# Prompt scores of two heads on two halves of the tensor array, with one split of keys and queries per pair

## The chip, the cores and the metric

The kernel runs on one core of one Trainium2 chip. The time is device microseconds of one execution; the number compared is the median of several runs. A profile of one execution gives the start and length of nearly every instruction on the five engines: TensorE (PE, with PEld for its weight loads), VectorE (DVE), ScalarE (ACT), GpSimd (POOL) and SyncE (SP, which here only issues DMAs).

## The reference

The reference is one inference step of a two-layer streaming encoder in float32: a convolution layer with its SwiGLU feed-forward, then a shared key/value projection, an attention layer with 16 heads of 64 features, a second feed-forward and a final norm. There are 512 new prompt frames and 8 running streams of 16 frames. The part that matters here is the attention of the prompt frames:

```python
def one_chunk(args):
    c, q_blk = args
    start = c * CHUNK
    k_blk = lax.dynamic_slice_in_dim(kp, start, BAND, axis=1)
    v_blk = lax.dynamic_slice_in_dim(vp, start, BAND, axis=1)
    s = jnp.einsum("bqhd,bkhd->bhqk", q_blk, k_blk).astype(jnp.float32) * scale + bias
    valid = (start - BAND_LEFT + jnp.arange(BAND)) >= 0
    s = jnp.where(valid[None, None, None, :], s, NEG_INF)
    p = jax.nn.softmax(s, axis=-1).astype(v_blk.dtype)
    return jnp.einsum("bhqk,bkhd->bqhd", p, v_blk)
```

For 512 frames in chunks of 64 with eight chunks to the left this is causal attention by chunks: each 128-frame tile of queries i (0 to 3) meets the keys 0 to (i+1)*128.

## The kernel before, in words

All matrix products run in the one-pass float32 format (`F32R`). To keep float32 accuracy each operand is split into a high part (rounded by a copy on ACT) and a low part (the difference, taken on DVE), and a product is the sum of high-high, high-low and low-high. In the projections and the feed-forwards that is three matmuls per tile (`mm3`, lines 196 to 202, and `product`, line 439).

The heads are worked on in eight pairs p. A tile of 128 partitions holds the keys of both heads of a pair, head 0 in partitions 0 to 63 and head 1 in 64 to 127 (`kts[p]`), and another the queries (`qts[p]`). They come from `proj_kq` (line 1200), the values from `proj_v` (line 1222, one call for two pairs).

`head_a(p, hh)` (line 1259) computes the prompt scores of one head and their softmax. Since a head has only 64 features, it fills all 128 rows of the array by stacking. `KK` holds the high part of the keys twice, once in each half of the partitions (an ACT copy at line 1271, then a POOL copy to the other half at line 1273). `KL` holds the low part twice (two DVE subtractions, line 1275). `QQ` holds the high part of the queries in one half (ACT, line 1272) and the low part in the other (DVE, line 1277). Then for each query tile, in the order 3, 2, 0, 1, two matmuls over all 128 rows give the sum of all four part products: `QQ` with `KK` (line 1285) and `QQ` with `KL` (line 1286). Widths are 512, 384, 128 and 256 columns. `KK`, `KL` and `QQ` have one buffer each (`KB = 1`). The scores of tiles 3, 2 and 0 go to one two-bank PSUM tile of the pool `w2` (`wide`), those of tile 1 into a spare part of a second one (`st`), which afterwards takes the scores of the sample streams. The pool `w2` has two such tiles in all. `addmax` on DVE (line 1194) adds the bias and takes the row maximum; `softmax_rows` runs the exponentials on ACT (line 1187); line 1296 divides on DVE.

The other steps of a pair are: `samp_a` (sample scores against the cache, lines 1342 and 1345, 32 array columns per stream), `head_b` (transposes of the prompt weights, line 1309), `pair_c` (prompt weights times values, line 1326, 64 array columns per head), `samp_b` (transposes, lines 1358 and 1364), and `samp_c` (sample weights times values, lines 1378 and 1382, then a transpose at 1391). All of these but `samp_a` write into the PSUM pool `am`, which has two one-bank tiles. The string `BO` (line 67) gives the written order of a pair: a0 s0 a1 s1 b0 b1 t0 n0 p0 c0 d0 t1 n1 c1 d1; `BL` is that of the last pair, with parts of the output projection put between.

The order in which the engines really receive the instructions is made by the framework's scheduler. It takes, among the instructions that are ready on its own clock, the one written first, and hands out the buffers of a pool as they come free. So the projections for the next pair, written after the pair, fill TensorE wherever the attention of this pair is waiting. Within an engine the resulting order is fixed, and semaphores hold the dependencies.

Of the kernel before, what the change touches and what calls it, by code (L numbers as in the profile page):

```python
# [8 lines left out]
F32 = mybir.dt.float32  # L9
F32R = mybir.dt.float32r  # L10
I32 = mybir.dt.int32
AF = mybir.ActivationFunctionType
ALU = mybir.AluOpType
PSUM = bass.MemoryType.PSUM

P = 128
# [6 lines left out]
DH = 64  # L23
# [32 lines left out]
NXA, NXB = NB * SEG + HIST + HA, HIST + 320  # L56
SSQ = 'avavavaa'
SCUT = 8
CB, QB, KB = 8, 1, 1
NSTD = 3  # L60
NH = NT // 2
X11, X21, XT2, XT1, XT3, XT4, X22 = range(7)
# [20 lines left out]
def tile_trunk(ctx, tc, xT, vecs, hist, w_pw1, w_pw2, w_in0, w_out0, w_os0, w_in1, w_out1, w_os1,  # L83
               w_kq, w_v, w_o, rel, kc, vc, y_out, convp_out, convs_out, k_out, v_out):
    nc = tc.nc
# [15 lines left out]
    def nm(s):  # L101
        uid[0] += 1
        return f"{s}_{uid[0]}"

    def mmt(n=512):
        return mm.tile([P, n], F32, tag="mm", name=nm("mm"))

    def w2t():
        return w2.tile([P, 1024], F32, tag="w2", name=nm("w2"))
# [761 lines left out]
    def conv_pe(c, part):  # L871
        w4, xa, xb = x4s[c]
        pt = mmt()
        n = {"S": NB * SB, "A": HA, "B": NH}[part]
        for tg in range(8):
            r = 96 if tg == 7 else P
            for q in range(4):
                if part == "S":
                    mv = xa[0:r, q, 0:NSC].rearrange("p (s w) -> p s w", w=SEG)
# [7 lines left out]
            yield  # L887
        o = {"S": 0, "A": NB * SB, "B": NH}[part]
        to_y(c, o, n, pt, func=AF.Identity, bias=col(V_BDW, c))
# [231 lines left out]
    def amt():  # L1121
        return am.tile([P, 512], F32, tag="am", name=nm("am"))

    sp = at.enter_context(tc.tile_pool(name="sp", bufs=2))
    ap = at.enter_context(tc.tile_pool(name="ap", bufs=1))

    qbd = []
    for i in range(2):
        q = ap.tile([P, NB, 2, SB], F32, name=f"qbd{i}", tag=f"qbd{i}")
# [11 lines left out]
    for b in range(4):  # L1141
        for hh in range(2):
# [3 lines left out]
                                      ap=[[0, 16], [2 * L, NP]]))  # L1146
# [33 lines left out]

    def softmax_rows(S, mx, sm, tiles):
        k = len(tiles)
# [15 lines left out]
    fill, step_end = None, [None]  # L1198
# [57 lines left out]

    ORD = (3, 2, 0, 1)

    def head_a(p, hh):
        kt, qt = kts[p], qts[p]  # L1260
        r = slice(hh * DH, hh * DH + DH)
        S = sp.tile([P, 1280], F32, tag="S", name=nm("S"))
        mx = ap.tile([P, 4], F32, tag="mx", name=nm("mx"), bufs=3)
        sm = ap.tile([P, 4], F32, tag="sm", name=nm("sm"), bufs=3)
        wide = w2t()
        st = w2t()
        ro = slice(DH - hh * DH, 2 * DH - hh * DH)
        KK = ap.tile([P, 512], F32R, tag="KK", name=nm("KK"), bufs=KB)
        KL = ap.tile([P, 512], F32R, tag="KL", name=nm("KL"), bufs=KB)
        QQ = ap.tile([P, 512], F32R, tag="QQ", name=nm("QQ"), bufs=KB)  # L1270
        nc.scalar.activation(out=KK[r], in_=kt[r, P:], func=AF.Copy)
        nc.scalar.activation(out=QQ[r], in_=qt[r, P:], func=AF.Copy)
        nc.gpsimd.tensor_copy(KK[ro], KK[r].bitcast(F32))
        for to in (r, ro):
            nc.vector.tensor_tensor(out=KL[to], in0=kt[r, P:], in1=KK[r].bitcast(F32),
                                    op=ALU.subtract)
        nc.vector.tensor_tensor(out=QQ[ro], in0=qt[r, P:], in1=QQ[r].bitcast(F32),
                                op=ALU.subtract)
        pss = []
        for i in ORD:  # L1280
            n = (i + 1) * P
            o = SOFF[i]
            q = slice(i * P, (i + 1) * P)
            ps = st[:, 640:896] if i == 1 else wide[:, o:o + n]
            nc.tensor.matmul(ps, QQ[:, q], KK[:, 0:n], start=True, stop=False)
            step_end[0] = nc.tensor.matmul(ps, QQ[:, q], KL[:, 0:n], start=False, stop=True).ins
            pss.append(ps)
        for ii, i in enumerate(ORD):
            n = (i + 1) * P
            o = SOFF[i]  # L1290
            addmax(S[:, o:o + n], pss[ii], BP[:, hh, 512 - n:512], mx[:, ii:ii + 1])
        rs = softmax_rows(S, mx, sm, [(SOFF[i], (i + 1) * P) for i in ORD])
        for ii, i in enumerate(ORD):
            n = (i + 1) * P
            o = SOFF[i]
            nc.vector.tensor_scalar(out=S[:, o:o + n], in0=S[:, o:o + n],
                                    scalar1=rs[:, ii:ii + 1], scalar2=None, op0=ALU.mult)
        return S, st

    def head_b(S):  # L1300
        PT = sp.tile([P, 1280], F32, tag="PT", name=nm("PT"))
        for kk in ((0,), (1, 3), (2,)):
            tr = amt()
            base = POFF[kk[0]]
            tot = 0
            for k in kk:
                for i in range(k, 4):
                    o = POFF[k] - base + (i - k) * P
                    step_end[0] = nc.tensor.transpose(
                        tr[:, o:o + P], S[:, SOFF[i] + k * P:SOFF[i] + (k + 1) * P], ident).ins  # L1310
                    tot += P
            if kk[0] == 0:
                nc.scalar.activation(out=PT[:, base:base + tot], in_=tr[:, :tot], func=AF.Copy)
            else:
                nc.vector.tensor_copy(PT[:, base:base + tot], tr[:, :tot])
        return PT
# [14 lines left out]
    def samp_a(p, u, st):  # L1331
        qb, kt = qbd[p % 2], kts[p]
        cache = []
        for src in (kc[p, u], vc[p, u].rearrange("p b k d -> p b (k d)")):
            for i in range(2):
                t = ap.tile([P, 2, 512], F32, tag="cache", name=nm("cache"), bufs=CB)
                nc.sync.dma_start(t, src[:, 2 * i:2 * i + 2, :])
                cache.append(t)
        KC, VC = cache[:2], cache[2:]
        qv = [qb[:, 4 * u + b, :, :].rearrange("p h q -> p (h q)") for b in range(4)]  # L1340
        for b in range(4):
            nc.tensor.matmul(st[32 * b:32 * b + 32, 0:512], qv[b], KC[b // 2][:, b % 2, :],
                             start=True, stop=True)
        for b in range(4):
            step_end[0] = nc.tensor.matmul(st[32 * b:32 * b + 32, 512:576], qv[b],
                                           kt[:, 64 * u:64 * u + 64], start=True, stop=True).ins
        S = ap.tile([P, 576], F32, tag="Ss", name=nm("Ss"), bufs=2)
        mx = ap.tile([P, 4], F32, tag="mx", name=nm("mx"), bufs=3)
        sm = ap.tile([P, 4], F32, tag="sm", name=nm("sm"), bufs=3)
        addmax(S, st[:, 0:576], BS, mx[:, 0:1])  # L1350
        rs = softmax_rows(S, mx, sm, [(0, 576)])
        return S, rs, VC
# [65 lines left out]
    for p in range(NP):  # L1418
        bias_load(p)
        if p < NP - 1:  # L1420
            oT[p] = (op_.tile([P, NT], F32R, tag="ohi", name=nm("ohi"), bufs=3),
                     op_.tile([P, NT], F32R, tag="olo", name=nm("olo"), bufs=3))
        else:
            oT[p] = (op_.tile([P, NT], F32, tag="kt", name=nm("ohi"), bufs=2).bitcast(F32R),
                     op_.tile([P, NT], F32, tag="qt", name=nm("olo"), bufs=QB).bitcast(F32R))
        ha, sa, pt, ps = {}, {}, {}, {}
        for op in (BL if p == NP - 1 else BO).split():
            i = int(op[1])
            if op[0] == "a":
                ha[i] = head_a(p, i)  # L1430
            elif op[0] == "s":
                sa[i] = samp_a(p, i, ha[i][1])
            elif op[0] == "b":
                pt[i] = head_b(ha[i][0])
            elif op[0] == "t":
                ps[i] = samp_b(i, sa[i][0])
            elif op[0] == "n":
                ps[i] = ps[i]()
            elif op[0] == "c":
                ps[i] = samp_c(p, i, ps[i], *sa[i][1:])  # L1440
            elif op[0] == "d":
                ps[i]()
            elif op[0] in "oq":
                if fill is None:
                    fill = halves(i, (mmt,), [])
                for _ in range(1 + (op[0] == "o")):
                    with tc.issue_after(step_end[0]):
                        next(fill)
            else:
                pair_c(p, (pt[0], pt[1]))  # L1450
        if p + 1 < NP:
            run(proj_kq(p + 1))
        if p % 2 == 1 and p + 1 < NP:
            run(proj_v(p // 2 + 1))
        if p in PO:
            proj_o(PO[p])
# [6 lines left out]
    with tc.high_priority(offset=HP):  # L1463
        sqs = xp.tile([P, KT, 384], F32, tag="xl1", name=nm("sqs")).rearrange("p a n -> p (a n)")
        acc, r = sqs[:, KT * NH:(KT + 1) * NH], sqs[:, (KT + 1) * NH:(KT + 1) * NH + 8]
        for k in range(KT):
            sq = square(h[:, k, 0:NH], NH, "a", sqs[:, k * NH:(k + 1) * NH])
            if k:
                sq_end = nc.vector.tensor_tensor(out=acc, in0=acc if k > 1 else sqs[:, 0:NH],
                                                 in1=sq, op=ALU.add).ins  # L1470
    for _ in range(MEAN_AT):
        next(fin)
    with tc.issue_after(half_end[0]), tc.high_priority(offset=HP):
        st, nt = w2t(), len(tiles(NH))
        for t, c in enumerate(tiles(NH)):
            end = nc.tensor.matmul(st[:, 512 + t:513 + t], acc[:, c:c + P], onec, start=True,
                                   stop=True)
# [109 lines left out]
    with tc.high_priority(offset=HP):  # L1587
        squares(0)
        st = mmt()
# [98 lines left out]
```

## Time and profile before

| what | value |
|---|---|
| median of 3 runs | 1460.51 us (1458.16 to 1463.31) |
| the profiled execution, its span | 1460.0 us |
| TensorE busy | 1434.0 us (98%) |
| VectorE busy | 1138.9 us (78%) |
| ScalarE busy | 757.8 us (52%) |
| GpSimd busy | 297.6 us (20%) |
| granted TensorE clock | 0.999 |

The page gives no time of the profiled execution beyond its span. Busy time is the union of the instructions' intervals; matmuls overlap their neighbours in the pipeline, so that the length of one matmul is longer than its share, and the distance between two starts is the better measure of its cost. A form such as `128*64 128x512` on a matmul means 128 array rows by 64 array columns in use and an output 512 wide. The attention stage runs from about 690 to 1005 us.

### The profile page before, as it was taken

How to read it: one execution, taken by the hardware profiler on the slowest of the kernel's cores; microseconds unless marked ns; L12 is line 12 of the kernel's file. 1: busy time of each engine (PE TensorE's matmuls, PEld its weight loads, DVE VectorE, ACT ScalarE, POOL GpSimd, SP SyncE). 2: the span in 40 equal slices, each digit the busy share in tenths (PEclk: the TensorE clock that was granted, in tenths of full speed). 3: DMA queues.
4: the chain of work that ended last, by engine and by line, in shares of the span. 5: the costliest groups of instructions: out<-in, count | busy, mean ns of one | idle time of the engine just before them, and what ended most of it. 6: DMA issues, size and time to landing. Idle time of an engine off the chain costs nothing. (4 is left out here: it accounts for less than half of the span.)

```text
span 1460.0 us, 28194 instructions
## 1 busy us (share of the span) xinstructions
PE 1434.0 (98%) x11022; PEld 1369.6 (94%) x11022; DVE 1138.9 (78%) x2520; ACT 757.8 (52%) x1628; POOL 297.6 (20%) x349
## 2 busy tenths in 40 slices
PE   9999999999999999999999999999999999999998
PEld 8998799999999999999987898878999999999998
DVE  6789867988888888756768668577898888888765
ACT  4666554654554554545654355443554564455453
POOL 5699120010111111013222121011011111111101
PEclk9999999999999999999999999999999999999999
DMA  7267434045444534425556554452125444444522
GB/s 243 73 180 187 126 86 146 14 135 150 131 108 118 163 92 135 116 88 193 181 163 213 173 192 162 138 200 67 44 82 143 135 113 129 137 120 109 155 66 72
DMA packets 66932, 192.56 MB, mean 132 GB/s; under 512 B 12144, under 2 KB 30320, under 8 KB 58480
## 3 DMA queue, kind: packets, MB, share of 16 engines
q1 hardware_dynamic: 52432, 160.58, 33.8%
q0 software_dynamic: 13504, 29.37, 9.9%
q8 instruction: 86, 1.41, 0.4%
q10 hardware_dynamic: 864, 0.83, 0.2%
q14 instruction: 46, 0.38, 0.1%
HBM read 179.14 MB, written 11.61 MB: 131 GB/s over the span
## 5 line engine op out<-in xcount | busy, mean ns | idle before, releaser
L439 PE MATMUL mm<-XH,whi 128*128 128x320 f32 x896 | 275.9, 310 | 2.9 <-ACT t L451 2.6
L439 PE MATMUL mm<-XH,wlo 128*128 128x320 f32 x896 | 276.1, 309 | 0.0
L439 PE MATMUL mm<-XL,whi 128*128 128x320 f32 x896 | 274.5, 309 | 0.0
L371 ACT ACTIVATE whi<-raw 128x512 fp32r<-128x512 f32 (+2 forms) x280 | 168.4, 613 | 135.2 <-PE mm L439 103.6
L199 PE MATMUL mm<-xh,whi 128*128 128x320 f32 (+2 forms) x640 | 200.2, 314 | 0.8 <-DVE h L702 0.4
L200 PE MATMUL mm<-xh,wlo 128*128 128x320 f32 (+2 forms) x640 | 198.2, 311 | 0.0
L372 DVE TENSOR_TENSOR wlo<-raw,whi 128x512 fp32r<-128x512 f32 (+2 forms) x280 | 183.9, 666 | 15.9 <-ACT whi L371 14.8
L201 PE MATMUL mm<-xl,whi 128*128 128x320 f32 (+2 forms) x640 | 195.9, 311 | 0.4 <-DVE xl L189 0.4
L439 PE MATMUL mm<-hid,whi 128*128 128x320 f32 x732 | 172.5, 311 | 5.5 <-DVE hid L372 3.1
L439 PEld LDWEIGHTS mm<-XH,whi 128*128 128x128 f32 x896 | 167.7, 188 | 4.9 <-ACT t L451 4.2
L439 PEld LDWEIGHTS mm<-XH,wlo 128*128 128x128 f32 x896 | 168.2, 188 | 0.0
L439 PEld LDWEIGHTS mm<-XL,whi 128*128 128x128 f32 x896 | 167.7, 188 | 0.0
L439 PEld LDWEIGHTS mm<-hid,whi 128*128 128x128 f32 x732 | 125.0, 188 | 8.8 <-DVE hid L372 4.2
L199 PEld LDWEIGHTS mm<-xh,whi 128*128 128x128 f32 x640 | 120.5, 188 | 4.0 <-ACT xh L187 1.5
L201 PEld LDWEIGHTS mm<-xl,whi 128*128 128x128 f32 x640 | 119.7, 188 | 1.2 <-DVE xl L189 0.8
L200 PEld LDWEIGHTS mm<-xh,wlo 128*128 128x128 f32 x640 | 120.5, 189 | 0.2
L439 PE MATMUL mm<-hid,wlo 128*128 128x320 f32 x366 | 113.0, 309 | 0.0
L439 PE MATMUL mm<-XH,slo 128*128 128x320 f32 x344 | 106.0, 308 | 0.0
L439 PE MATMUL mm<-XH,shi 128*128 128x320 f32 x344 | 105.8, 309 | 0.0
L439 PE MATMUL mm<-XL,shi 128*128 128x320 f32 x344 | 105.6, 308 | 0.0
L417 POOL DMA_DIRECT2D s<-in_w_in x38 | 22.1, 581 | 388.7 <-DVE wlo L372 151.8
L841 POOL TENSOR_TENSOR ca<-ca,cvt 128x512 f32<-128x512 f32 x60 | 91.9, 1532 | 17.8 <-ACT cvt L838 11.2
(275 smaller groups left out, 3370.8 us busy)
## 6 DMA issues: line engine op xcount, KB each, us to landing
raw<-in_w_in SPq DMA_DIRECT2D x38, 1024.0 KB
s<-in_w_in POOLq DMA_DIRECT2D x76, 256.0 KB, 4.2
raw<-in_w_os SPq DMA_DIRECT2D x24, 768.0 KB
cache<-in_ck SPq DMA_DIRECT2D x32, 512.0 KB
cache<-in_cv SPq DMA_DIRECT2D x32, 512.0 KB
raw<-in_w_pw SPq DMA_DIRECT2D x11, 1024.0 KB
s<-in_w_os POOLq DMA_DIRECT2D x48, 192.0 KB, 3.6
raw<-in_w_kq SPq DMA_DIRECT2D x8, 1024.0 KB
```

The costliest lines, as they stand in the source:

```text
L199: nc.tensor.matmul(ps, wh, xh, start=(first and i == 0), stop=False)
L200: nc.tensor.matmul(ps, wl, xh, start=False, stop=False)
L201: end = nc.tensor.matmul(ps, wh, xl, start=False, stop=(stop and i == last))
L371: put_end[1] = nc.scalar.activation(out=hi, in_=src, func=AF.Copy).ins
L372: put_end[0] = nc.vector.tensor_tensor(out=lo, in0=src, in1=hi.bitcast(F32), op=sub).ins
L417: nc.gpsimd.dma_start(s1, src[:, 2 * n:3 * n])
L439: last = nc.tensor.matmul(pt, wt, v, start=(first and k == i == 0), stop=(k == n - 1 and i == 2), skip_group_check=True)
L841: nc.gpsimd.tensor_tensor(out=acc, in0=acc, in1=pr, op=ALU.add)
```

## The change

`head_a` is cut in two. A new function `heads_split(p)` is called once per pair, ahead of head 0. It splits the keys and the queries of both heads in one go, over all 128 partitions: two ACT copies, two DVE subtractions, nothing on POOL. Then it issues the scores of both heads: per query tile three matmuls per head (high-high, low-high, high-low), each over the 64 rows of its head, the two heads taking turns. The low-low product is no longer computed. Head 0 uses rows 0 to 63 of the array, head 1 rows 64 to 127. The scores of tiles 3, 2 and 0 go to two `w2` tiles, one per head, and those of tile 1 to two tiles of the pool `am`. The sample scores get a `w2` tile of their own when their turn comes. `head_a` keeps the bias, the maximum and the softmax.

```diff
-CB, QB, KB = 8, 1, 1
+CB, QB = 8, 1
...
-    def head_a(p, hh):
+    def heads_split(p):
         kt, qt = kts[p], qts[p]
-        r = slice(hh * DH, hh * DH + DH)
-        S = sp.tile([P, 1280], F32, tag="S", name=nm("S"))
-        mx = ap.tile([P, 4], F32, tag="mx", name=nm("mx"), bufs=3)
-        sm = ap.tile([P, 4], F32, tag="sm", name=nm("sm"), bufs=3)
-        wide = w2t()
-        st = w2t()
-        ro = slice(DH - hh * DH, 2 * DH - hh * DH)
-        KK = ap.tile([P, 512], F32R, tag="KK", name=nm("KK"), bufs=KB)
-        KL = ap.tile([P, 512], F32R, tag="KL", name=nm("KL"), bufs=KB)
-        QQ = ap.tile([P, 512], F32R, tag="QQ", name=nm("QQ"), bufs=KB)
-        nc.scalar.activation(out=KK[r], in_=kt[r, P:], func=AF.Copy)
-        nc.scalar.activation(out=QQ[r], in_=qt[r, P:], func=AF.Copy)
-        nc.gpsimd.tensor_copy(KK[ro], KK[r].bitcast(F32))
-        for to in (r, ro):
-            nc.vector.tensor_tensor(out=KL[to], in0=kt[r, P:], in1=KK[r].bitcast(F32),
-                                    op=ALU.subtract)
-        nc.vector.tensor_tensor(out=QQ[ro], in0=qt[r, P:], in1=QQ[r].bitcast(F32),
-                                op=ALU.subtract)
-        pss = []
+        KH, KL, QH, QL = (ap.tile([P, 512], F32R, tag=t, name=nm(t)) for t in ("KH", "KL", "QH", "QL"))
+        for src, hi, lo in ((kt, KH, KL), (qt, QH, QL)):
+            nc.scalar.activation(out=hi, in_=src[:, P:], func=AF.Copy)
+            nc.vector.tensor_tensor(out=lo, in0=src[:, P:], in1=hi.bitcast(F32), op=ALU.subtract)
+        wide = [w2t(), w2t()]
+        narrow = [amt(), amt()]
+        pss = [[], []]
         for i in ORD:
             n = (i + 1) * P
             o = SOFF[i]
             q = slice(i * P, (i + 1) * P)
-            ps = st[:, 640:896] if i == 1 else wide[:, o:o + n]
-            nc.tensor.matmul(ps, QQ[:, q], KK[:, 0:n], start=True, stop=False)
-            step_end[0] = nc.tensor.matmul(ps, QQ[:, q], KL[:, 0:n], start=False, stop=True).ins
-            pss.append(ps)
+            for hh in range(2):
+                pss[hh].append(narrow[hh][:, 0:n] if i == 1 else wide[hh][:, o:o + n])
+            for j, (a, b) in enumerate(((QH, KH), (QL, KH), (QH, KL))):
+                for hh in range(2):
+                    r = slice(hh * DH, hh * DH + DH)
+                    step_end[0] = nc.tensor.matmul(pss[hh][-1], a[r, q], b[r, 0:n], start=j == 0,
+                                                   stop=j == 2).ins
+        return pss
+
+    def head_a(p, hh, pss):
+        S = sp.tile([P, 1280], F32, tag="S", name=nm("S"))
+        mx = ap.tile([P, 4], F32, tag="mx", name=nm("mx"), bufs=3)
+        sm = ap.tile([P, 4], F32, tag="sm", name=nm("sm"), bufs=3)
...
-        return S, st
+        return S
...
             if op[0] == "a":
-                ha[i] = head_a(p, i)
+                if i == 0:
+                    pss = heads_split(p)
+                ha[i] = head_a(p, i, pss[i])
             elif op[0] == "s":
-                sa[i] = samp_a(p, i, ha[i][1])
+                sa[i] = samp_a(p, i, w2t())
             elif op[0] == "b":
-                pt[i] = head_b(ha[i][0])
+                pt[i] = head_b(ha[i])
```

## The prediction

> **What bounds the kernel now.** I read the page first: shares of busy time, then the slices.
>
> ```profile
> span 1460.0 us, 28194 instructions
> ...
> PE 1434.0 (98%) x11022; PEld 1369.6 (94%) x11022; DVE 1138.9 (78%) x2520; ACT 757.8 (52%) x1628; POOL 297.6 (20%) x349
> ...
> PE   9999999999999999999999999999999999999998
> ...
> PEclk9999999999999999999999999999999999999999
> ```
>
> TensorE is busy in every slice and its clock is never cut. The attention stage is no exception; the view of busy time by stretches gives it one row (stretch, its length, then busy time of PE, PEld, DVE, ACT and POOL):
>
> ```profile
> 690.00:1005.00 315.00, 310.25 (x2798) 270.23 (x2797) 218.71 (x654) 157.73 (x424) 57.27 (x95) 1.00 0.51 169
> ```
>
> So 4.75 of 315 us are left uncovered on TensorE, with DVE at 69% and ACT at 50%. What the change takes from DVE, ACT and POOL can pay only through these few microseconds; what it does to TensorE's own time counts in full. That is the first cut of the sum. The timeline of TensorE shows the scores of one head (start, length, line, form):
>
> ```profile
> 763.14 0.39 PE L1285 MATMUL w<-KK,QQ 128*128 128x512 f32 x1
> 763.38 0.40 PE L1286 MATMUL w<-KL,QQ 128*128 128x512 f32 x1
> 763.61 0.34 PE L1285 MATMUL w<-KK,QQ 128*128 128x384 f32 x1
> 763.78 0.34 PE L1286 MATMUL w<-KL,QQ 128*128 128x384 f32 x1
> 763.96 0.22 PE L1285 MATMUL w<-KK,QQ 128*128 128x128 f32 x1
> 764.02 0.27 PE L1286 MATMUL w<-KL,QQ 128*128 128x128 f32 x1
> 764.13 0.33 PE L1285 MATMUL w<-KK,QQ 128*128 128x256 f32 x1
> 764.30 0.28 PE L1286 MATMUL w<-KL,QQ 128*128 128x256 f32 x1
> 764.42 0.28 PE L199 MATMUL mm<-xh,whi 128*128 128x256 f32 x1
> ```
>
> The reader should look at the distances of the starts. A matmul costs 0.235 us at 512 columns (763.14 to 763.61, halved), 0.175 at 384, and 0.12 at 256 (764.30 to 764.42). At 128 columns the first takes 0.06 and the next 0.11. I read 0.11 as the floor that a weight load sets when each narrow matmul needs new weights, and 0.17 for the first 256 as the same load arriving late. The head takes 764.42 - 763.14 = 1.28 us, a pair 2.56, eight pairs 20.5 us: 1.4% of the span is all that the change can touch directly on TensorE.
>
> **The change on TensorE.** Per pair 16 matmuls over 128 rows go, 24 over 64 rows come. If the two heads, on different halves of the rows and in different PSUM banks, run at the same time, a pair of them costs one distance, and a query tile three: 3 x (0.235 + 0.175 + 0.11 + 0.12) = 1.92 us instead of 2.56. If they run one after another it is twice that, 3.84. No row of before has both row halves at work, so these are the two bounds. The nearest rows are the sample scores, four streams on four column quarters:
>
> ```profile
> 699.94 0.28 PE L201 MATMUL mm<-xl,whi 128*128 128x256 f32 x1
> 700.06 0.28 PE L199 MATMUL mm<-xh,whi 128*128 128x256 f32 x1
> 700.27 1.07 PE L1342 MATMUL w<-cache,qbd 128*32 128x512 f32 x8
> 701.16 0.29 PE L1345 MATMUL w<-kt,qbd 128*32 128x64 f32 x8
> 701.38 0.39 PE L200 MATMUL mm<-xh,wlo 128*128 128x256 f32 x1
> 701.60 0.28 PE L201 MATMUL mm<-xl,whi 128*128 128x256 f32 x1
> ```
>
> ```profile
> 700.27 0.16 PEld L1342 LDWEIGHTS w<-cache,qbd 128*32 128x32 f32 x8
> ```
>
> Eight matmuls of 512 columns take 701.16 - 700.27 = 0.89 us, where eight in a row would take 8 x 0.235 = 1.88 at the least, and their eight weight loads start within a fraction of a microsecond. Parts of the array do work at once in this kernel. I take the overlap, 1.92, since this is the nearest row, and keep 3.84 for the range.
>
> The same rows price the second term: going into a divided array and out of it. Before the sample scores the distance is 700.27 - 700.06 = 0.21 instead of the 0.12 just ahead: 0.09 lost. After them, the 64-column round starts at 701.16 and lasts two rounds of 0.89 / 2 / 8 = 0.056, so 0.11 of the 0.22 to 701.38 are lost; and the first whole-array matmul takes 0.22 instead of 0.12, another 0.10. One trip costs about 0.30 us. Today's scores are whole-array work like the projections around them and pay nothing of the kind. So the number of blocks into which the scheduler cuts the 24 matmuls decides the sign: one block gives 1.92 + 0.30 - 2.56 = -0.34 per pair, -2.7 us in all; two give -0.04 and -0.3 us; three give +0.26 and +2.1 us.
>
> I take two. The last query tile is written into `am`, whose two tiles also serve all transposes and both value products, so it has to wait for these to be emptied while the tiles 3, 2 and 0 are free to go. Already now, the last width is cut off by projections when its PSUM tile comes late:
>
> ```profile
> 772.78 0.28 PE L1286 MATMUL w<-KL,QQ 128*128 128x128 f32 x1
> ...
> 774.32 0.28 PE L1285 MATMUL w<-KK,QQ 128*128 128x256 f32 x1
> ```
>
> A third block is possible because the high-high matmuls need only the two ACT copies and can be issued ahead of the DVE subtractions. A trip next to the sample work, which has already divided the array, would cost less; I leave that at nothing.
>
> **The change on the other engines.** From the groups by line and shape (count | busy, mean ns of one | idle before):
>
> ```profile
> L1275 DVE TENSOR_TENSOR KL<-kt,KK 64x512 fp32r<-64x512 f32 x32 | 24.0, 749 | 4.9 <-ACT KK L1271 4.5
> L1277 DVE TENSOR_TENSOR QQ<-qt,QQ 64x512 fp32r<-64x512 f32 x16 | 11.0, 685 | 1.1 <-ACT QQ L1272 0.9
> L372 DVE TENSOR_TENSOR wlo<-raw,whi 128x512 fp32r<-128x512 f32 x30 | 20.3, 683 | 1.0 <-ACT whi L371 0.9
> L1272 ACT ACTIVATE QQ<-qt 64x512 fp32r<-64x512 f32 x16 | 9.8, 615 | 0.0
> L371 ACT ACTIVATE whi<-raw 128x512 fp32r<-128x512 f32 x30 | 18.4, 628 | 9.5 <-PE mm L439 8.5 <-DVE h L580 0.6 <-DVE raw L425 0.4
> L1273 POOL CAST KK<-KK 64x512 fp32r<-64x512 f32 x16 | 14.3, 894 | 127.4 <-ACT KK L1271 126.0 <-issue 1.3
> ```
>
> A half-height subtraction costs as much as a whole one. Per pair DVE drops 4 x 0.749 + 2 x 0.685 = 4.37 us and gains 2 x 0.683 = 1.37: 3.0 us less, 24 us over the stage. ACT goes from about 4 x 0.62 to 2 x 0.628, 1.2 us less per pair. POOL loses both copies, and with them the wait on ACT at the head of its queue, behind which the bias scaling of the next pair stood. No DMA is added or moved. All of this lies beside TensorE; its worth is bounded by the waits that TensorE really has. The timeline shows the larger ones (in brackets: idle, and on whom):
>
> ```profile
> 752.58 0.39 PE L199 MATMUL mm<-whi,xh 128*128 128x256 f32 x1 [0.52 <-ACT vt L1234]
> ...
> 794.87 0.44 PE L1309 MATMUL am<-ident,S 128*128 128x128 f32 x2 [0.41 <-DVE PT L1315]
> 795.70 0.66 PE L1358 MATMUL am<-ident,Ss 128*128 128x128 f32 x4 [0.39 <-ACT PT L1313]
> ```
>
> ```profile
> L1285 PE MATMUL w<-KK,QQ 128*128 128x512 f32 x16 | 7.0, 440 | 1.3 <-DVE QQ L1277 1.2
> ```
>
> These add up to 0.52 + 0.41 + 0.39 + 1.2 = 2.5 us. That is the upper bound of the relief.
>
> Against it stands a new wait. Both `am` tiles are held from the last score matmul until head 1's last `addmax`. Behind them wait the transposes, the value products and, through those, the output projection. One head's four `addmax` run like this:
>
> ```profile
> 733.03 0.69 DVE L1194 CUSTOM_DVE_ANT_0 S<-w,BP 128x512 f32<-128x512 f32 x1 [0.92 <-PE w L1286]
> ...
> 734.68 0.08 DVE L1194 DVE_READ_ACCUMULATOR2_ANT mx<- 128x1 f32 x1
> ```
>
> That is 1.73 us, so 3.46 for two heads. The sample scores wait too: their `w2` tile is free only after the head's first three `addmax`. Head 1's scores now stand ahead of the first sample scores on TensorE; before they came after them. The cover for all this is the projections of the next pair:
>
> ```profile
> L199 PE MATMUL mm<-xh,whi 128*128 128x384 f32 x112 | 38.7, 346 | 0.0
> L199 PE MATMUL mm<-whi,xh 128*128 128x256 f32 x142 | 40.6, 286 | 0.5 <-ACT vt L1234 0.5
> ```
>
> Each line stands for three matmuls, so these two groups alone are 112 x 3 x 0.175 + 142 x 3 x 0.12 = 110 us, 13.7 per pair, against 3.46 to be hidden. I cost the hold at nothing while they are there, the relief at nothing as well, and keep +13.8 us (half of the hold bare in each pair) and -2.5 us for the range.
>
> **The sum.** Profiled 1460.0, two blocks per pair -0.3: 1459.7. The median of the runs lies 0.5 above the profiled span, so **1460.2 us**: no change that could be measured. About 0.3%, or 4.4 us, is what runs of this kernel can tell apart.
>
> **Rivals.** First, the halves do not overlap. For it speaks that no row shows both at work, against it the column quarters. With two trips a pair takes 3.84 + 0.60 instead of 2.56: 8 x 1.88 = 15.0 us, **1475.5**; with one trip 12.6, 1473.1.
>
> Second, slower by the hold: the scheduler places the last tile's scores ahead of the previous pair's value product, and that product then waits for two heads of `addmax` with no projection between. It decides from the point where TensorE's next instruction needs an `am` tile and the projections have run dry. Half the hold bare costs 8 x 1.73 = 13.8: **1474**. Against it: 13.7 us of cover per pair; for it: the waits at 794.87 and 795.70, where it already happens in small.
>
> Third, the overlap is partial: the matmuls overlap, but the weight loads of the two halves follow one another at 0.11 each, so no pair of matmuls is under 0.22. Then 3 x (0.235 + 3 x 0.22) = 2.69, plus 0.60, less 2.56: +0.73 per pair, **1466.3**; with one trip 1463.9. For it speaks the 0.11 floor above, against it the eight loads at 700.27. [...]
>
> Fourth, faster: one block per pair (-2.7) and all of TensorE's listed waits gone (-2.5): **1455.3**. For it: 24 us less on DVE; against it: the `am` tiles.
>
> **How the numbers follow.** Forecast 0.50, with its own range 1456.5 to 1464 (one block and some relief, to three blocks and a little waiting). Not overlapping 0.13, the hold 0.16, partial overlap 0.07, faster 0.14. Faster by over 0.3% (under 1456.1) takes most of the fourth rival and a sliver of the forecast: 0.15. Slower by over 0.3% (over 1464.9) takes the first rival, most of the second and third, and an edge of the forecast: 0.34. Within: 0.51. The range 1455 to 1475 cuts through the first rival and the fourth and leaves about 0.15 out.
>
> **What would show it.** Rows `64*128` on TensorE whose starts come in twos, a few ns apart, with the next two 0.235 us later at 512 columns, show the overlap; equal distances of 0.235 refute it. At 128 columns, 0.11 per two says that loads overlap, 0.22 that they do not. Projections between `64*128` rows count the blocks. Idle time of lines 1309 and 1326 put down to line 1194 would show the hold. I would be wrong if TensorE's uncovered time in the stage grew from 4.75 us to over 9, or if the scores of a pair, trips included, left the span of 2.2 to 2.8 us.

## The result and the profile after

The changed kernel takes 1478.92 us (median of 4 runs, 1476.75 to 1479.29); the kernel before took 1460.95 us beside it (4 runs, 1458.16 to 1463.31). The ratio is 1.0126 with a 95% interval of 1.0114 to 1.0138: 18 us slower. The forecast was 1460.2 us with a range of 1455 to 1475, so the forecast and its range were both wrong.

The page of the changed kernel, beside the one shown of before (span, busy time by engine):

```profile
span 1474.9 us, 28213 instructions
...
PE 1446.4 (98%) x11086; PEld 1370.6 (93%) x11086; DVE 1119.6 (76%) x2488; ACT 746.1 (51%) x1612; POOL 282.3 (19%) x333
```

TensorE is busy for 12.4 us more and the span is 14.9 us longer; the profiled execution is the fastest of the four, so that the profile shows a little less than the 18 us. DVE and ACT did become lighter (by 19.3 and 11.7 us), and no run shows that it bought anything. The row of busy time for the attention stage of the changed kernel:

```profile
690.00:1020.00 330.00, 321.81 (x2842) 270.18 (x2841) 193.79 (x615) 144.49 (x400) 44.67 (x80) 0.99 0.48 158
```

Uncovered time is 330.00 - 321.81 = 8.19 us, where it was 4.75. From the first score matmul to the start behind the last attention matmul the stage took 307.8 us before (694.8 to 1002.6) and takes 325.1 us now (692.6 to 1017.7). It begins 2.2 us earlier and ends 15.1 us later, which is the whole difference of the spans. So TensorE's own time rose by far more than its idle time. The timeline of the changed kernel shows the scores of the first pair (start, length, line, form, count):

```profile
692.37 0.28 PE L201 MATMUL mm<-wlo,xh 128*128 128x256 f32 x1
692.58 0.50 PE L1277 MATMUL w<-KH,QH 64*128 64x512 f32 x2
...
693.03 0.40 PE L1277 MATMUL w<-KH,QL 64*128 64x512 f32 x2
693.26 0.39 PE L1277 MATMUL w<-KL,QH 64*128 64x512 f32 x2
693.49 0.33 PE L1277 MATMUL w<-KH,QH 64*128 64x384 f32 x2
693.66 0.34 PE L1277 MATMUL w<-KH,QL 64*128 64x384 f32 x2
...
694.07 0.28 PE L1277 MATMUL w<-KH,QL 64*128 64x128 f32 x2
694.19 0.27 PE L1277 MATMUL w<-KL,QH 64*128 64x128 f32 x2
694.30 0.33 PE L1277 MATMUL am<-KH,QL 64*128 64x256 f32 x2
694.47 0.28 PE L1277 MATMUL am<-KL,QH 64*128 64x256 f32 x1
694.67 0.39 PE L199 MATMUL mm<-whi,xh 128*128 128x256 f32 x1
...
697.74 0.38 PE L1277 MATMUL am<-KL,QH 64*128 64x256 f32 x1
```

Each row with x2 is the two heads, and the next row comes 0.23 us later at 512 columns, 0.17 at 384 and 0.12 at 128 (693.03 to 693.26, 693.49 to 693.66, 694.07 to 694.19). The kernel before has 0.235, 0.175 and 0.11 for one matmul over the whole array (763.14 to 764.13), so the halves run at the same time. From 692.58 to 694.67 23 of the pair's 24 matmuls cost 2.09 us, and 2.28 with the 0.09 lost ahead of them and the 0.10 behind, against 2.56 before: up to here the change does what it was meant to do. But the last matmul of one head comes alone, at 697.74, and costs another 0.51 us with the trip around it (697.53 to 698.28, less the 0.24 of two projections). And this first pair is the best of the eight. Here is the second pair:

```profile
723.19 0.28 PE L201 MATMUL mm<-xl,whi 128*128 128x256 f32 x1
723.40 0.50 PE L1277 MATMUL w<-KH,QH 64*128 64x512 f32 x2
723.83 0.44 PE L199 MATMUL mm<-xh,whi 128*128 128x384 f32 x1
...
728.22 0.50 PE L1277 MATMUL w<-KH,QL 64*128 64x512 f32 x2
...
729.48 0.28 PE L1277 MATMUL w<-KL,QH 64*128 64x128 f32 x2
729.69 0.44 PE L199 MATMUL mm<-xh,whi 128*128 128x384 f32 x1
...
743.47 0.33 PE L1388 MATMUL am<-ident,os 128*128 128x128 f32 x1
743.73 0.38 PE L1277 MATMUL am<-KH,QH 64*128 64x256 f32 x1
...
747.59 0.28 PE L201 MATMUL mm<-wlo,xh 128*128 128x256 f32 x1
747.80 0.38 PE L1277 MATMUL am<-KH,QH 64*128 64x256 f32 x1
748.02 0.28 PE L1277 MATMUL am<-KH,QL 64*128 64x256 f32 x1
748.14 0.28 PE L1277 MATMUL am<-KL,QH 64*128 64x256 f32 x1
748.35 0.39 PE L199 MATMUL mm<-whi,xh 128*128 128x256 f32 x1
748.57 0.28 PE L200 MATMUL mm<-whi,xl 128*128 128x256 f32 x1
```

The pair's scores are in four blocks instead of one. The two high-high matmuls go alone, ahead of the subtractions (723.40); 0.43 us pass until the next start, for work worth 0.23. Then come tiles 3, 2 and 0 (728.22 to 729.69). The last tile, in `am`, comes 14 us later, one head at a time: head 0 right behind line 1388, the last transposes of the previous pair, and head 1 another 4.07 us later. Two heads that start 4 us apart overlap nothing. The block at 747.80 also shows what one trip costs: the distance ahead of it is 0.21 instead of 0.12, that of its first matmul 0.22, that of its last 0.21, and that of the first whole-array matmul 0.22. Together 0.38 us are lost. This pattern of the last tile repeats in seven of the eight pairs, in six of them with other work between the heads.

Counted over the timeline of the stage, there are 34 blocks of scores (23 before), 4.25 per pair; TensorE goes from one way of dividing the array to another 170 times (103 before); and the scores take 25.7 us from start to start (21.3 before), 3.2 us per pair instead of 2.66. The groups of waits of TensorE in this stage (engine, tile, line, awaited: us in total, times, longest):

```profile
PE am L1306 <- DVE PT L1312: 1.8, 4, 0.8
PE w L1339 <- DMA cache<-in_ck: 1.7, 1, 1.7
...
PE am L1277 <- DVE mx L1194: 0.5, 1, 0.5
```

No wait stands out. The one that the forecast named, for `addmax` (line 1194), is 0.5 us in all.

### The profile page after: what moved, and what is told of

It reads as the page before. It is cut to its first block, busy times and chain, and to the rows that moved or that the text cites. A ratio compares the mean times of both kernels' runs of the same rounds, so it can differ in the third digit from the quotient of the medians.

```text
span 1474.9 us, 28213 instructions
## 1 busy us (share of the span) xinstructions
PE 1446.4 (98%) x11086; PEld 1370.6 (93%) x11086; DVE 1119.6 (76%) x2488; ACT 746.1 (51%) x1612; POOL 282.3 (19%) x333
```

## The experiments

The two theories of the expectations: **A**, the loss is the price of the divided array, the trips into and out of it; **B**, the loss is the last tile's place in `am`, which ties the scores to the tail of the previous pair. The stage is again measured from the first score matmul to the start behind the last attention matmul; it begins at 691.1 to 696.8 us, latest in e6 and e10. Uncovered time is that of TensorE from 690 to 1035 us, the same stretch for all, which takes in a little of the next stage. The kernel before was run beside each group of runs and took 1459.0 to 1459.8 us (1460.95 beside the change).

| kernel | median us | ratio to before (95%) | stage us | changes of the array's division | score blocks | uncovered us |
|---|---|---|---|---|---|---|
| before | 1460.95 | | 307.8 | 103 | 23 | 5.5 |
| the change | 1478.92 | 1.0126 (1.0114 to 1.0138) | 325.1 | 170 | 34 | 8.6 |
| e1_am | 1486.84 | 1.0190 (1.0175 to 1.0205) | 334.7 | 112 | 21 | 21.2 |
| e2_half_st | 1469.47 | 1.0071 (1.0056 to 1.0086) | 317.7 | 157 | 31 | 8.5 |
| e3_trips | 1478.06 | 1.0131 (1.0113 to 1.0148) | 327.1 | 205 | 24 | 3.7 |
| e5_one_block | 1490.15 | 1.0209 (1.0191 to 1.0226) | 340.6 | 128 | 13 | 23.4 |
| e8_mm_plain | 1469.00 | 1.0065 (1.0050 to 1.0080) | 316.6 | 145 | 27 | 10.3 |
| e6_mm_block | 1469.49 | 1.0068 (1.0051 to 1.0085) | 313.8 | 124 | 13 | 12.9 |
| e10_mm_first | 1468.69 | 1.0063 (1.0048 to 1.0078) | 313.6 | 114 | 13 | 14.1 |
| e11_whole | 1466.83 | 1.0059 (1.0044 to 1.0074) | 314.4 | 108 | 25 | 12.5 |
| e12_mm_whole | 1460.50 | 1.0006 (0.9997 to 1.0016) | 309.4 | 116 | 22 | 7.6 |

**e3_trips: what a trip costs.** The kernel before, with one tiny matmul over 64 rows behind each tile's scores, 64 in all:

```diff
             pss.append(ps)
+            nc.tensor.matmul(st[:, 960:964], QQ[0:DH, q], KK[0:DH, 0:4], start=True, stop=True)
```

> The kernel before with 64 matmuls added, one after each query tile's two score matmuls of each head, over 64 rows and 4 columns wide, into a spare part of the sample tile; nobody reads them. Each is a trip into the row-divided array and back. It measures the price of a trip: at the 0.30 us read off the column-divided rows, 64 trips cost 19 us, 1480 us in all. Theory A expects 1475 to 1485; if a trip between whole rows and half rows costs far less than one to columns (theory B), the time stays under 1468.

Measured 1478.06 us, 18.3 more than the 1459.77 of before beside it. The timeline of e3_trips:

```profile
693.53 0.40 PE L1286 MATMUL w<-KL,QQ 128*128 128x512 f32 x1
693.86 0.27 PE L1288 MATMUL w<-KK,QQ 64*128 64x4 f32 x1
694.06 0.44 PE L1285 MATMUL w<-KK,QQ 128*128 128x384 f32 x1
694.34 0.34 PE L1286 MATMUL w<-KL,QQ 128*128 128x384 f32 x1
```

The way in costs 0.33 - 0.235 = 0.095, the tiny matmul itself 0.20, and the first whole-array matmul behind it 0.28 - 0.175 = 0.105 too much: 0.40 in all, with the tiny matmul in it. The 64 added matmuls made 102 more changes of the division, not 128. So the 18.3 us are 0.18 for each change, and the 19.3 us by which the stage grew are 0.19: a trip of two changes costs 0.36 to 0.38, as in the block at 747.80 of the changed kernel. How much of it is the tiny matmul's own, this run does not separate. A trip into row halves costs somewhat more than the 0.30 that the forecast had read from the column quarters; above all it was the number of trips that was wrong.

**e1_am: the last tile in `am`, the array not divided.** The kernel before, whose last tile goes to `am`:

```diff
-        st = w2t()
+        narrow = amt()
...
-            ps = st[:, 640:896] if i == 1 else wide[:, o:o + n]
+            ps = narrow[:, 0:n] if i == 1 else wide[:, o:o + n]
...
-                sa[i] = samp_a(p, i, ha[i][1])
+                sa[i] = samp_a(p, i, w2t())
```

> The kernel before with one part of the change alone: the scores of the last query tile go to a tile of the pool am and the sample scores get a w2 tile of their own; all scores stay whole-array, each head is split and scored by itself. Theory A (the extra 18 us are trips into and out of the divided array, and matmuls of one head that run alone): no trip is added, so the time stays at that of before, 1461 us within 3. Theory B (the am tiles held by the scores make TensorE wait): most of the loss is here, 1470 us or more, and TensorE's idle time in the attention stage grows from 4.75 us to over 8.

Measured 1486.84 us, 27 more than before, with next to no added changes of the array (112 against 103). So a place in `am` can cost this much with no divided array at all, and A alone falls. But the size can't be carried over. In this kernel `KK`, `KL` and `QQ` have one buffer each, so when head 0's last tile waits for `am`, head 1's split waits for head 0's operands. Its waits of TensorE:

```profile
PE w L1285 <- POOL BP L1154: 4.7, 1, 4.7
PE w L1285 <- POOL BP L1157: 4.7, 1, 4.7
```

These two, 9.4 us, are waits that the changed kernel doesn't have. Its granted clock is down too, to 0.97 on the mean from 690 to 1035 us, which costs up to 0.03 x 345 = 10 us. This run is no clean measure.

**e2_half_st: the change, with the last tile back in the sample's tile.** The last tile's three half-row matmuls are issued per head in `head_a`, into the spare part of that head's second `w2` tile:

```diff
-    def head_a(p, hh, pss):
+    def head_a(p, hh, pss, parts):
+        QH, KH, QL, KL = parts
+        st = w2t()
+        r = slice(hh * DH, hh * DH + DH)
+        pss = pss + [st[:, 640:896]]
+        for j, (a, b) in enumerate(((QH, KH), (QL, KH), (QH, KL))):
+            step_end[0] = nc.tensor.matmul(pss[-1], a[r, P:2 * P], b[r, 0:256], start=j == 0,
+                                           stop=j == 2).ins
```

> The changed kernel, but the scores of the last query tile go back to the w2 tile that the sample scores use, so that am is left to the transposes and value products as before. In the written order the scheduler makes 31 blocks of score matmuls out of 34, and each head's last tile is still alone in its block. Theory A: the number of trips hardly falls, so the time stays near 1477 us (1474 to 1480). Theory B: the waits go, the time falls to 1466 us or less.

Measured 1469.47 us: half of the loss is gone, though the last tile now never overlaps its partner by construction. The division still changes 157 times. Neither theory alone covers this: if trips were all, 13 changes fewer would be worth some 2 us; if `am` were all, the time would be back at before.

**e5_one_block: fewest trips.** The change, with the scores held together as one block per pair. The last tile goes first, the low-high term leads, and the other 23 matmuls may be issued only after the first:

```diff
-        for i in ORD:
+        for i in (1, 3, 2, 0):
...
-            for j, (a, b) in enumerate(((QH, KH), (QL, KH), (QH, KL))):
-                for hh in range(2):
+            for j, (a, b) in enumerate(((QL, KH), (QH, KH), (QH, KL))):
+                for hh in (1, 0):
+                    with tc.issue_after(gate) if gate else nullcontext():
```

> The changed kernel with the score matmuls kept together: the last-width tile is scored first, its first matmul needs the low part of the queries (the last thing split), and all other score matmuls of the pair come behind it. In the scheduled order there are 13 blocks instead of 34, nearly one per pair, and all matmuls come in twos. It still holds am, for all the longer since both tiles must be free before any score. Theory A: 21 trips fewer at 0.30 are 6.3 us, and the last tile overlapping again is worth 7 x 0.36 = 2.5 us: 1470 us or less. Theory B: no better than the changed kernel, 1478 us or more, with idle TensorE time in the stage over 10 us.

Measured 1490.15 us, the slowest of all, with 42 changes fewer than the changed kernel. TensorE's row of 690 to 1035 us for e5_one_block:

```profile
690.00:1035.00 345.00, 321.56 (x2842) 274.55 (x2841) 192.53 (x618) 145.06 (x402) 39.88 (x78) 0.95 0.45 153
```

and its waits:

```profile
PE w L1343 <- issue: 3.4, 3, 1.5
PE am L1392 <- DVE os L1388: 3.4, 6, 0.9
PE am L1278 <- DVE olo L189: 3.3, 2, 2.5
```

Uncovered are 23.4 us, 17.9 more than before, and the granted clock falls to 0.95 on the mean, which costs up to another 0.05 x 345 = 17 us. Together that is about the 32.8 us by which the stage is longer than before. When all 24 matmuls wait for `am`, the pair's scores come only after the previous pair's tail, and there is not enough other work left to fill the gap. The cut blocks of the changed kernel were the cheaper of the two ways to pay for `am`.

**e8_mm_plain and e6_mm_block: the last tile in the projections' pool.** e8 is the change with one word different; e6 is e5 with the same word:

```diff
-        narrow = [amt(), amt()]
+        narrow = [mmt(), mmt()]
```

> The changed kernel with one word changed: the last tile's scores go to the two tiles of the projections' pool mm instead of am. Order of the score matmuls as written in the change; the scheduler makes 27 blocks of them instead of 34, and two heads' last tiles come together in most pairs. Theory A (trips): 7 trips fewer at 0.29 to 0.36 us and some overlap regained, 1478.9 - 4 = 1475 us. Theory B (scores tied to am lengthen the chain of the pair, and TensorE waits): the 9 us that the sample-tile version gained are had here too, 1470 us or less.

> As the kernel kept in one block per pair (13 blocks, last tile first), but with the last tile's scores in mm instead of am. Theories A and B both have their remedy here: trips 1478.9 - 7 - 2.5 (21 trips fewer, overlap of the last tile regained), am waits another 5 less: 1462 to 1466 us. If it stays above 1475, holding the projections' own tiles makes TensorE wait as much as am did. Compared with the 1490 of the same order in am, the difference is what am alone costs when the scores wait for it first.

Measured 1469.00 and 1469.49 us. Out of `am`, the changed kernel regains 9.9 us and the single block 20.7. The stretch of 690 to 1035 us for e8_mm_plain:

```profile
690.00:1035.00 345.00, 334.68 (x2993) 288.96 (x2992) 216.35 (x664) 158.09 (x425) 47.30 (x82) 1.00 0.47 160
```

Uncovered time did not fall (10.3 against 8.6 us): what `am` had cost the changed kernel was not idle time on TensorE but TensorE's own time. 25 changes fewer are 4.5 us at 0.18 and 4.8 at 0.19; the half clock that the changed kernel shows in its last pair (below) is another 1.5; 36 instead of 44 of the last tile's matmuls run alone, 4 distances of 0.12, 0.5 us. That is 6.5 to 6.8 us; the stage became 8.5 us shorter although 1.7 more of the stretch is uncovered, so some 3.5 us stay unplaced. Between e8 and e6 21 changes are saved (3.8 to 4.0 us), and the time is the same, above the 1462 to 1466 expected of e6. The largest group of waits in e6_mm_block says where part of it went:

```profile
PE mm L1278 <- ACT vt L1234: 4.1, 3, 1.7
```

A block that must not be cut waits with all of TensorE for its first PSUM tile (4.1 us in three waits). The granted clock is also at half for two stretches of 3.4 us in e6 (from 860.25 and 952.41; 0.99 on the mean from 690 to 1035 us), and never in this stage of e8 (1.00).

**e10_mm_first: is the held `mm` tile what costs?** e6, with both heads' last tile passed to `addmax` first, so that the `mm` tiles come free early:

```diff
+        for hh in range(2):
+            addmax(S[:, SOFF[1]:SOFF[1] + 256], pss[hh][3], BP[:, hh, 256:512], mx[:, 3:4])
```

> The same one-block kernel in mm, but DVE adds the bias and takes the maximum of the last tile of both heads ahead of all others, so that the projections get their two tiles back after about 0.9 us of DVE work instead of 3.5. If the held mm tiles are what still costs, it gains 1 to 4 us on the run before, towards 1460; if not, the two are equal within 1.5 us.

Measured 1468.69 us, 1468.09 to 1469.50, where e6 has 1468.69 to 1470.97. The two can't be told apart, so when the held tile is let go does not matter here; the wait for `vt` to leave its `mm` tile is there again (5.7 us in four waits).

**e11_whole and e12_mm_whole: the array not divided, all else as changed.** In the change (e11) and in e8 (e12) the 24 half-row matmuls of a pair become 12 over all rows, with the same widths, tiles and splits:

```diff
-            for j, (a, b) in enumerate(((QH, KH), (QL, KH), (QH, KL))):
-                for hh in range(2):
-                    r = slice(hh * DH, hh * DH + DH)
-                    step_end[0] = nc.tensor.matmul(pss[hh][-1], a[r, q], b[r, 0:n], start=j == 0,
-                                                   stop=j == 2).ins
+            for hh, a, b, first in ((0, QH, KH, True), (1, QL, KH, True), (0, QH, KL, False)):
+                step_end[0] = nc.tensor.matmul(pss[hh][-1], a[:, q], b[:, 0:n], start=first,
+                                               stop=hh == 1 or not first).ins
```

By the distances of the kernel before, 12 whole matmuls have the price that 12 perfectly overlapping pairs would have, 3 x (0.235 + 0.175 + 0.11 + 0.12) = 1.92 us per pair. What is missing against the changed kernel is what dividing costs, as far as the scheduler leaves the rest in its order.

> The changed kernel with its 24 half-row matmuls per pair replaced by 12 over all 128 rows (per query tile two for head 0, one for head 1). They take 3 x (0.235 + 0.175 + 0.11 + 0.12) = 1.92 us per pair, as much as 24 that overlap perfectly, but there is no trip into the divided array and no matmul alone. The rest, splits, PSUM tiles, am, softmax, is as changed. Left out: the scores are no longer those of the heads (they mix both heads, and parts of the products are missing), so only the time counts. If trips and lone matmuls are 67 array changes at 0.145 to 0.18 us and 2.5 us, it takes 1478.9 - 12 to 14.5 = 1464 to 1467 us. If the waits that come with am are nearly all of the loss, it stays above 1474.

> The same replacement in the version with the last tile's scores in mm (1469.0 us, 145 array changes against 103 of the kernel before). The same part of the computation is left out. With both causes gone, trips and am, and the scores 0.64 us per pair cheaper than in the kernel before, it should come to 1460 to 1464 us: 42 array changes at 0.145 to 0.18 are 6 to 7.5 us. Under 1457 would mean that the relief of DVE, ACT and POOL is worth something; above 1466 that a third cause is left.

Measured 1466.83 and 1460.50 us (e12 with 10 runs). With these the four cases are complete:

| last tile in | halves of the array | whole array | cost of dividing |
|---|---|---|---|
| `am` | 1478.9 | 1466.8 | 12.1 |
| `mm` | 1469.0 | 1460.5 | 8.5 |
| cost of `am` | 9.9 | 6.3 | 18.4 together |

Here `am` is measured against `mm` and not against no cost at all. Each cause alone makes the kernel slower, and without both it is level with before. The medians come from different groups of runs; by the ratios to the kernel before beside each, dividing costs 9.8 us with `am` and 8.6 with `mm`, `am` costs 8.9 with halves and 7.7 on the whole array, and together they cost 17.5. The 3.6 us by which the medians make each dearer beside the other shrink to 1.2, less than the 1.4 to 2.2 us by which each ratio is uncertain, so that this is not shown. On the whole array `am` costs in another coin. The stretch of 690 to 1035 us for e11_whole:

```profile
690.00:1035.00 345.00, 332.48 (x2914) 289.67 (x2914) 217.75 (x672) 159.13 (x431) 48.97 (x82) 0.99 0.48 162
```

and for e12_mm_whole:

```profile
690.00:1035.00 345.00, 337.37 (x2948) 294.49 (x2948) 223.09 (x676) 164.27 (x437) 51.19 (x82) 1.00 0.48 164
```

There `am` is 4.9 us of uncovered time (12.5 against 7.6), with no more changes of the division (108 against 116). One wait of e11_whole is nearly as much:

```profile
PE w L1275 <- ACT KH L1263: 4.5, 1, 4.5
```

The last matmul that reads the old `KH` (one buffer) runs at 787.03; the key split of the next pair then stands on ACT behind weight splits until 791.27, and the scores start at 791.94. Behind this wait (790.45 to 797.28), and once more from 978.18 to 981.60, the clock is at half: 10.2 us in all, against 3.4 in e12_mm_whole.

e12 also prices the rest of the change. It has the single split for both heads, nothing on POOL, and scores that should cost 0.64 us less per pair, 5.1 in all; yet it is level with before, 1.0006. Its stage is 1.6 us longer (its profiled execution, 1462.60 us, was 2.1 over the median), with 13 more changes of the division (2.3 to 2.5 us), 2.1 us more uncovered, and a stretch of 3.4 us at half clock from 720.38 that before lacks, worth about 1.5: 5.9 to 6.1 of the 6.7 us between the gain it should bring and what came. The rest was not pursued. The relief of DVE, ACT and POOL can't be seen in any run.

## Why the prediction was wrong

**What bounds the kernel: right.** TensorE's own time decided. The two busy engines that were relieved gave nothing back, as the first cut of the sum had it.

**The halves overlap, 1.92 us per pair: right.** The distances are 0.23, 0.17, 0.12 and 0.17 or 0.12 for a pair of matmuls, and the weight loads of the two halves overlap as well (last section). The first rival (no overlap, 1475.5) and the third (partial overlap, 1466.3) fall, though the time is nearer to theirs. Two halves of 64 rows take the 0.23 us of one whole matmul at 512 columns (693.03 to 693.26), with nothing lost.

**One trip 0.30 us: a fifth too low.** It is 0.38 in the block at 747.80 and 0.36 to 0.38 in e3_trips. The forecast priced three places from the rows of the sample scores; a fourth, the first matmul in the divided array, loses another 0.10.

**"I take two": the first step that failed.** There were 4.25 blocks per pair, 34 in all, and the 67 more changes of the division are nearly these 34 ways in and out. By the prediction's own formula 4.25 blocks are 1.92 + 4.25 x 0.30 - 2.56 = +0.64 us per pair, +5.1 in all, instead of -0.3. To this comes what the formula had no term for: a cut not only adds a trip, it can part the two heads. 44 of the last tile's 48 matmuls ran alone, 22 distances of 0.12 more, 2.6 us. That is 7.7 us more than before at 0.30 a trip, and 10.4 at 0.38. Against the same kernel on the whole array, dividing measured 8.5 us (e8 against e12) and 9.8 to 12.1 (the change against e11). The text had seen both reasons for a cut (the late `am` tile, the high-high term ahead of the subtractions), and took them for one cut and a possible second. It did not ask whether the two `am` tiles come free at the same time. They come free one after the other, 4.07 us apart in the second pair, with each step of the previous pair's tail.

**"I cost the hold at nothing while they are there": the second step that failed.** `am` costs 8.9 to 9.9 us with halves and 6.3 to 7.7 on the whole array, against `mm`. The cover was real: 0.5 us of waiting of the scores for `addmax` is all that the trace shows, and the projections filled the time. But the sum looked at the wrong side of the tile. It priced what waits behind the scores that hold `am`; the larger price is that the scores wait for `am`, behind the previous pair's transposes and value products. And the cover is not free for a divided array: each time a projection fills a gap between the scores, that is a trip. The second rival (1474) had this place and about the right size, by another mechanism, bare `addmax`, which did not occur.

**The relief at nothing: right in size.** No run shows more.

**The sum with what was measured:** 67 changes at 0.18 to 0.19 are 12.1 to 12.7 us, overlap -5.1, lone matmuls +2.6, uncovered time 8.19 - 4.75 = +3.4, half clock +1.5: 14.5 to 15.1 of the 17.3 by which the stage grew. The rest of 2 to 3 us is not placed.

**The marks that the prediction set:** one of the two came. The scores of a pair take 3.2 us, outside of 2.2 to 2.8. Uncovered time stayed at 8.19, under the bound of 9, so this mark would have passed a kernel that is 18 us slower: on an engine that is full, a count of instructions by form and a count of changes say more than idle time does. The idle time of lines 1309 and 1326 that was to betray the hold is not there either; the hold shows as cuts.

## What to carry to other kernels

Where a scheduler fills gaps, price work on a divided array by its blocks and not only by its matmuls: 0.38 us for each block here, and nothing saved when the partner halves are issued apart. Before an early step of the next unit is put into a pool through which the last steps of this unit pass in turn, ask when each tile of the pool comes free for it, not only how long it will hold one. Holding the block together by hand does not help while its first tile is late: TensorE then waits for it, with all the work that is ordered behind (23.4 us uncovered in e5_one_block, 8.6 in the changed kernel).

## What the runs showed of the hardware

The granted clock fell to half (0.51) in the changed kernel's last pair. The rows of three stretches, two ahead of the fall and the one behind it (start and end, length, busy time of PE, PEld, DVE, ACT and POOL, granted clock, DMA share, GB/s):

```profile
984.22:987.63 3.41, 1.67 (x23) 0.86 (x17) 2.44 (x10) 0.99 (x3) 0.00 (x0) 1.00 0.78 271
...
991.05:994.46 3.41, 2.41 (x20) 1.77 (x13) 2.31 (x10) 1.35 (x5) 0.00 (x0) 1.00 0.02 7
994.40:997.80 3.40, 3.40 (x15) 3.40 (x14) 2.90 (x12) 3.40 (x12) 0.00 (x0) 0.51 0.03 7
```

And the timeline of TensorE ahead of it and in it (idle time and its releaser in brackets):

```profile
987.59 1.05 PE L1339 MATMUL w<-cache,qbd 128*32 128x512 f32 x4 [1.74 <-DMA cache<-in_ck]
...
991.70 0.33 PE L1388 MATMUL am<-ident,os 128*128 128x128 f32 x1 [0.47 <-DVE os L1384]
...
993.11 0.38 PE L1277 MATMUL am<-KH,QH 64*128 64x256 f32 x1 [0.53 <-DVE mx L1194]
...
994.06 0.31 PE L201 MATMUL mm<-olo,whi 128*128 128x320 f32 x1
994.21 0.31 PE L199 MATMUL mm<-ohi,whi 128*128 128x320 f32 x1
...
995.04 0.47 PE L200 MATMUL mm<-ohi,wlo 128*128 128x320 f32 x1
995.31 0.47 PE L201 MATMUL mm<-olo,whi 128*128 128x320 f32 x1
```

At half clock TensorE has no gap, but a matmul of 320 columns costs 0.27 us (995.04 to 995.31), where it cost 0.15 just ahead (994.06 to 994.21). Over 3.4 us that loses 3.4 x (1 - 0.15 / 0.27) = 1.5 us. Behind the stretch, from 997.80 to 1001.20, the clock is at 0.99 again. Ahead of the half clock lies no gap longer than 1.74 us, but several short ones, the three in brackets among them. In the 3.41 us ahead of the fall TensorE was busy for 2.41, 71% by the trace. From 984.22 to 987.63, with the longest gap, it was busy for 1.67, and the clock stayed whole (1.00). So busy time alone does not tell when the clock falls; what decides it, these runs do not show. The two kernels with the most uncovered time from 690 to 1035 us have the lowest clock there: 0.95 on the mean with 23.4 us in e5_one_block and 0.97 with 21.2 in e1_am. The kernel before has 1.00 with 5.5, but e10_mm_first has 1.00 with 14.1 too.

A second point: the weight loads of the two halves run together too. Loads of the first pair, on PEld:

```profile
694.12 0.19 PEld L1277 LDWEIGHTS w<-KL,QH 64*128 64x128 f32 x2
```

The two loads are done within 0.19 us, and one load of the whole array takes 0.19 as well (692.25, line 201). At 128 columns the distance of 0.11 for one whole-array matmul was the distance of two half-row ones (694.19 to 694.30). The forecast read 0.11 as a floor set by the weight load. In the kernel before, the twelve matmuls of line 240 from 1036.66, one column wide and each with a load of the whole array, come (1.48 - 0.25) / 11 = 0.11 us apart too, so it is not the width that sets it there; that the load does is the author's reading.
